# Two of four weight sums of a seven-product quad made by accumulating DMA on the GpSimd queue, and activations in 4 KB tiles of one pool (hybrid RG-LRU / attention layer, Trainium2)

## The chip, the cores and the metric

The kernel runs on one core of one Trainium2 chip. The metric is the device time of one execution in microseconds (us), as the median of several runs. Of the core's engines, PE multiplies matrices, VectorE (DVE in the profile) and ScalarE (ACT) work elementwise, GpSimd (POOL) does a few masks and issues some DMAs, and SyncE (SP) issues nearly all DMAs.

## The reference

One layer of a decoder trunk, 256 rows of 2048 features in float32, with an FFN of 5632 hidden features:

```python
mod = (c_act @ ada_w[l] + ada_b[l])[:, None, :]
sh1, sc1, g1, sh2, sc2, g2 = jnp.split(mod, N_MOD, axis=-1)
h = modulate(rms_norm(x, norm1_g[l]), sh1, sc1)
proj = h @ w_in[l] + b_in[l]
u, lru_gate, q, k, v, mix_gates = jnp.split(proj, SPLITS, axis=-1)
...
merged = gate_lru * (y_lru @ w_lru_out[l]) + gate_attn * (y_attn @ w_attn_out[l])
x = x + g1 * (merged @ w_o[l])
h2 = modulate(rms_norm(x, norm2_g[l]), sh2, sc2)
gate, up = jnp.split(h2 @ w_ffn_in[l], 2, axis=-1)
x = x + g2 * ((jax.nn.silu(gate) * up) @ w_ffn_out[l])
return rms_norm(x, final_g)
```

The elided part is a causal convolution, a gated linear recurrence and windowed attention. The change touches only the FFN's two products, the gate `g2` that the FFN needs at its end, and the tiles in which `h`, `h2` and the last rows lie.

## The kernel before, in words

**Products.** Every float32 operand is split into a rounded part `hi` and a remainder `lo`, and a product is three matmuls: hi by hi, hi by lo and lo by hi (`mm3`, L355 to L357; in the last stage written out at L1352). A weight block comes from HBM into a tile `raw` (128 x 1024, 512 KB), ScalarE casts it to `hi` (L305), and VectorE subtracts to get `lo` (L317).

**Order.** The program's order on every engine is the order in which the Python code emits it. All products are entries of a list `items`, and `step(i)` (L328) emits for item i, in this order: the loads up to item i+5, the weight sums `made` up to item i+4, the casts up to item i+3, the `lo` splits up to item i+2, the stages in `before`, and then the item's own matmuls. Three `lo` tiles, four `hi` tiles and five `raw` tiles go round, so a split waits for the matmuls of the item three before it. Work that is not on this path (normalisation, modulation, recurrence, attention) is cut into generators (`posts`, `sides`) and put between the items by a small model of the engines' clocks.

**Quads of seven.** At some places four neighbouring blocks of weights (two of the contraction, two of the output) and four of the activations form a quad, and `seven` (L397) makes their product with seven block products instead of eight. This needs four sums of weight blocks, each 128 x 512, and four of the activations. Two further items of the list are these weight sums: `first` (L418, L419) subtracts two pairs of raw blocks, `second` (L424, L425) goes on from there. VectorE makes all four; the results go the way of a raw block, through a cast and a split. In the FFN's first product (`add_pair`, output slabs 1 to 10) three of the eight pairs of contraction blocks are quads; `made` takes the two tiles of the tag `araw`. In the FFN's last product (`seven_last`) there are eight quads in each half of the output, taken in turn with plain pairs; there the sums lie in the tile `last`, which also holds the final rows and gain.

**The FFN's gate.** `ada_rows` computes the row of `g2`: 32 loads `aw` (512 KB each), each multiplied and added into `pa` by VectorE (L688), and then four matmuls `pb` on PE that sum over the partitions (L694), copied back by ScalarE (L696). `aw` uses the same two `araw` tiles and up to a few spare tiles of the pool `bp`. It runs as a side, and `all_modulations` finishes it ahead of output slab 1. Slab 0 is made plainly, by two slabs of eight items each: `fg` (gate half) and `fu` (up half).

**Tiles.** `h` and later `h2` lie in one tile of 32 KB in a pool of its own (`hp`), and after them `last` (32 KB). Everything else of 4 KB a partition lies in the pool `bp`, with 25 tiles.

Of the kernel before, what the change touches and what calls it, by code (L numbers as in the profile page):

```python
# [43 lines left out]

N_K = 1
# [17 lines left out]
N_MADE, N_HOLD = 5, 4  # L63
SEVEN = tuple(range(6, 36, 4))

SEVEN_1, SLAB_7 = (4, 8, 12), 1
EARLY = NH - 2 * N_HOLD

# [6 lines left out]
def hybrid_layer(  # L75
# [8 lines left out]
    hp = ctx.enter_context(tc.tile_pool(name="hp", bufs=1))  # L84
    bp = ctx.enter_context(tc.tile_pool(name="bp", bufs=N_B4))
# [191 lines left out]

    items = []
    live = {}
    at = {"load": 0, "made": 0, "hi": 0, "lo": 0}  # L280

    def do_load(i):
        src, cols = items[i].src, items[i].cols
        if callable(src):
            live[i] = [None, None, None, 0.0]
            return
        raw = wp.tile([P, CH], F32, tag="raw", name=f"raw{i}", bufs=AHEAD - 1)
        nc.sync.dma_start(raw[:, :cols], src)
        live[i] = [raw, None, None, load_time(cols)]

    def do_made(i):
        src = items[i].src
        if callable(src):
            clock["dve"] = max(clock["dve"], live[i - 1][3])
            live[i][0] = src(i)
            charge(1.2, 0)
            live[i][3] = clock["dve"]
# [29 lines left out]
    def step(i):  # L327
# [68 lines left out]

    SUMS = 4  # L397

    def seven(loads, where, act, bank, begin, end, made_in, post=None):

        got = {}

# [8 lines left out]
        def block(k, n):  # L411
            l, c0 = where[k, n]
            return got[l][:, c0:c0 + 512]

        def first(i):
            got.update({0: live[i - 2][0], 1: live[i - 1][0]})
            x = got["x"] = made_in(0)
            nc.vector.tensor_tensor(x[:, 0:512], block(0, 1), block(0, 0), op=ALU.subtract)  # L418
            nc.vector.tensor_tensor(x[:, 512:], block(0, 1), block(1, 1), op=ALU.subtract)  # L419
            return x  # L420

        def second(i):
            y, x = made_in(1), got["x"]
            nc.vector.tensor_tensor(y[:, 0:512], block(1, 1), x[:, 0:512], op=ALU.subtract)  # L424
            nc.vector.tensor_tensor(y[:, 512:], block(1, 0), y[:, 0:512], op=ALU.subtract)  # L425
            return y

        plain = ((0, (0, 0), "p"), (1, (1, 0), "00"), (6, (1, 1), "01"))
        for l in range(2):
            jobs = [(a, where[kn][1], to) for a, kn, to in plain if where[kn][0] == l]  # L430
            cs = [c0 for _, c0, _ in jobs]
            items.append(Item(
                loads[l], CH, products(*jobs), weight=0.25 * len(jobs), used=(min(cs), max(cs) + 512),
            ))
        items.append(Item(first, CH, products((3, 0, "r"), (5, 512, "u")), weight=0.5))
        items.append(Item(second, CH, products((4, 0, "q"), (2, 512, "10")), post, weight=0.5))

    def sums_of(to, a11, a12, a21, a22):

        s1, s2, s3, s4 = (to[:, i, :] for i in range(SUMS))  # L440
        nc.vector.tensor_tensor(s1, a21, a22, op=ALU.add)
        nc.vector.tensor_tensor(s3, a21, a11, op=ALU.subtract)
        nc.vector.tensor_tensor(s2, s1, a11, op=ALU.subtract)
        nc.vector.tensor_tensor(s4, a12, s2, op=ALU.subtract)
# [63 lines left out]
    h_both = hp.tile([P, NK, 2, S], F32R, tag="h", name="h_both")  # L508
    h_hi, h_lo = h_both[:, :, 0, :], h_both[:, :, 1, :]

    def hact(kt):
# [4 lines left out]
        return h_hi[:, kt, :], h_lo[:, kt, :]  # L516
# [17 lines left out]
    def h_low(kt):  # L534
        nc.vector.tensor_tensor(h_lo[:, kt, :], hx[kt], f32(h_hi[:, kt, :]), op=ALU.subtract)
        h_done.add(kt)

    def modulated():
        for kt in range(2):
# [6 lines left out]
            nc.scalar.copy(h_hi[:, kt, :], hx[kt])  # L546
            yield 0.33, 0
            h_low(kt)
        for kt in range(2, NK):
# [6 lines left out]
            nc.scalar.copy(h_hi[:, kt, :], hx[kt])  # L556
# [540 lines left out]
    def second_norm(banks):  # L1097
        sides[:] = [ada_ffn]
        clock["slack"] = SLACK[1]
        both = h2["both"] = hp.tile([P, NK, 2, S], F32R, tag="h", name="h2_both")  # L1100
        hh, hl = both[:, :, 0, :], both[:, :, 1, :]
# [38 lines left out]
        def high(p):  # L1140
            for j in range(2):
                kt = 2 * p + j
                nc.scalar.activation(hh[:, kt, :], x1T[p][:, j, :], AF.Identity, bias=modc[:, 3, kt:kt + 1])

        def low(p):
            for j in range(2):
                kt = 2 * p + j
                nc.vector.scalar_tensor_tensor(
                    hl[:, kt, :], x1T[p][:, j, :], modc[:, 3, kt:kt + 1], f32(hh[:, kt, :]),
# [42 lines left out]
    def h2act(kt):  # L1192
        return h2["both"][:, kt, 0, :], h2["both"][:, kt, 1, :]
# [39 lines left out]
    def add_pair(s):  # L1233
# [24 lines left out]
        def shared():  # L1258
# [9 lines left out]
            nc.vector.tensor_tensor(x[:, 1, :], banks["r"], g[:, 1, :], op=ALU.add)  # L1268
            nc.vector.tensor_tensor(x[:, 0, :], banks["r"], x[:, 0, :], op=ALU.add)
# [19 lines left out]
        for k in range(0, NK, 2):  # L1289
            loads = [w_f1[s + 11 * n][:, k * 512:(k + 2) * 512] for n in range(2)]  # L1290
            if k in SEVEN_1:
                last = k == SEVEN_1[-1]
                seven(
                    loads, {(0, 0): (0, 0), (1, 0): (0, 512), (0, 1): (1, 0), (1, 1): (1, 512)}, act(k), bank,
                    k == SEVEN_1[0], last,
                    lambda i: wp.tile([P, CH], F32, tag="araw", name="made", bufs=N_ADA), shared if last else None,
# [4 lines left out]
        if s == SLAB_7:  # L1301
            items[start].before.append(all_modulations)
# [16 lines left out]
    def last_first():  # L1319
        ada_ffn.finish(streams[-1].fetch)  # L1320
        last = hp.tile([P, 4, D], F32, tag="h", name="last")
        fin["x2"], fin["fg"], fin["made"] = last[:, 0:2, :], last[:, 2, :], last[:, 3, :]
        fin["ss"] = const.tile([P, 2, 5], F32, name="ss3")

# [6 lines left out]
    def fetch_last():  # L1331
        yield 0, 0
        nc.sync.dma_start(fin["fg"], fg_row.partition_broadcast(P))
        for t in range(2):
            yield 0, 0
            nc.sync.dma_start(fin["x2"][:, t, :], x1d[rows(t), :])
# [23 lines left out]
    def seven_last(k, n, src):  # L1360
        parts = {}

        def parts_high():
            hi = parts[0] = wp.tile([P, 8, P], F32R, tag="araw", name=f"ah{n}_{k}", bufs=N_ADA)
# [8 lines left out]
        def own(to):  # L1373
# [9 lines left out]
            (src[k], src[k + 1]), {(0, 0): (0, 0), (0, 1): (0, 512), (1, 0): (1, 0), (1, 1): (1, 512)},  # L1383
            lambda a: [parts[h][:, a, :] for h in range(2)], own, k == SEVEN[0], k == SEVEN[-1],
            lambda i: fin["made"][:, i * CH:(i + 1) * CH], (lambda: combined(n)) if k == SEVEN[-1] else None,
        )

    def combined(n):
# [16 lines left out]
        nc.vector.tensor_tensor(pqr, fin["r"], pq, op=ALU.add)  # L1405
        nc.vector.tensor_tensor(pqur, fin["r"], pqu, op=ALU.add)
# [11 lines left out]
    def add_block(t, ps, c0, cols, dst=None):  # L1418

        x2 = fin["x2"][:, t, c0:c0 + cols]  # L1420
# [12 lines left out]
    def blocks(n0, n1):  # L1433

        def post():
# [10 lines left out]
            for t in range(2):  # L1446
# [3 lines left out]
                x2 = fin["x2"][:, t, n0 * 512:n1 * 512]  # L1450
                nc.vector.tensor_tensor(x2, x2, fin["fg"][:, n0 * 512:n1 * 512], op=ALU.mult)
# [26 lines left out]
    def finish_first():  # L1478
# [223 lines left out]
```

## Time and profile before

| | |
|---|---|
| runs | 1550.64, 1551.02 and 1556.88 us, median 1551.02 |
| the profiled execution | 1549.47 us |
| its span, first to last instruction | 1547.7 us, mean granted PE clock 0.997 |
| busy | PE 1530.9, PE weight loads 1314.2, VectorE 1392.2, ScalarE 858.2, POOL 3.7 us |
| DMA | 400.37 MB, 259 GB/s over the span |
| chain that ended last | PE 93%, DMA 4%, DVE 2%, issue 1% |

Rows of the trace give the start in us from the first instruction, the duration in us, the engine, the line and operation, the tile written and the tiles read, and in brackets how long the engine stood idle before and what ended that. PE's matmuls overlap in the profile (one of 128 x 512 shows 0.39 us but the next one starts 0.23 later), so PE is read by starts, not by busy time. PEld is PE's weight load. In grouped rows the columns after the count are busy us, mean ns, and idle time before.

### The profile page before, as it was taken

The page shows a single profiled execution, that of the slowest core. Times are in us where ns is not written, and L with a number is a line of the kernel's source. Part 1 is how long each engine was busy: PE and PEld are TensorE (multiplying, and loading weights), DVE is VectorE, ACT ScalarE, POOL GpSimd, SP SyncE. Part 2 cuts the span into 40 slices and gives each one's busy share as a digit, 9 for nine tenths or more (in the row PEclk, how much of TensorE's full clock was granted, in tenths as well). Part 3 has the DMA queues.
Part 4 walks back from the last instruction along what each step waited for, and adds up shares of the span by engine and source line. Part 5 has one row for each costly group of instructions (what it writes and reads, how often), then busy time and mean ns, then how long its engine had stood idle before and what let it go on. Part 6 is the DMA issues. An engine that isn't in the chain of part 4 may idle for free.

```text
span 1547.7 us, 22116 instructions
## 1 busy us (share of the span) xinstructions
PE 1530.9 (99%) x8013; PEld 1314.2 (85%) x8013; DVE 1392.2 (90%) x1854; ACT 858.2 (55%) x1113; POOL 3.7 (0%) x11
## 2 busy tenths in 40 slices
PE   8999999999999999999999999999999999999997
PEld 7999999998878887888888788888888888888786
DVE  7889989889888887988988899999999999998998
ACT  4654443776855445444545655555555556664664
POOL 0000000000000000000000000000000000000000
PEclk9999999999999999999999999999999999999999
DMA  9999998666887797999999665565555666766563
GB/s 367 343 320 345 341 315 291 212 203 208 270 275 264 259 328 274 368 339 339 366 384 346 191 202 187 194 198 200 200 192 200 207 193 236 251 206 204 189 212 128
DMA packets 112909, 400.37 MB, mean 259 GB/s; under 512 B 12432, under 2 KB 12576, under 8 KB 112416
## 3 DMA queue, kind: packets, MB, share of 16 engines
q1 hardware_dynamic: 112192, 397.39, 74.5%
q8 instruction: 62, 1.02, 0.3%
q0 software_dynamic: 320, 1.06, 0.2%
q10 hardware_dynamic: 288, 0.52, 0.1%
q14 instruction: 47, 0.39, 0.1%
HBM read 394.72 MB, written 4.20 MB: 258 GB/s over the span
## 4 chain that ended last, share of the span: by engine, by line
PE 93%; DMA 4%; DVE 2%; issue 1%; ACT 0%; SPq 0%; DVEq 0%; ACTq 0%
PE pf L1352 9%; PE f L356 7%; PE f L357 7%; PE f L355 7%; PE wi L357 6%; PE wi L355 6%; PE wi L356 6%; PE wga L357 2%; PE wga L355 2%; PE wga L356 2%; PE wa L357 2%; PE wa L355 2%; PE wa L356 2%; PE wl L356 2%; PE wl L357 2%; PE wl L355 2%
## 5 line engine op out<-in xcount | busy, mean ns | idle before, releaser
L305 ACT CAST hi<-raw 128x1024 fp32r<-128x1024 f32 (+1 forms) x540 | 536.9, 1002 | 447.3 <-PE wi L356 77.2
L317 DVE TENSOR_TENSOR lo<-raw,hi 128x1024 fp32r<-128x1024 f32 (+1 forms) x540 | 618.7, 1159 | 66.0 <-issue 35.0
L357 PE MATMUL wi<-h_both,lo 128*128 128x256 f32 x800 | 227.3, 284 | 3.6 <-DVE lo L317 3.6
L355 PE MATMUL wi<-h_both,hi 128*128 128x256 f32 x800 | 228.0, 285 | 0.0
L356 PE MATMUL wi<-h_both,hi 128*128 128x256 f32 x800 | 227.0, 284 | 0.0
L355 PE MATMUL f<-hi,h_both 128*128 128x512 f32 x460 | 180.2, 392 | 0.0
L357 PE MATMUL f<-hi,h_both 128*128 128x512 f32 x460 | 179.0, 389 | 0.0
L356 PE MATMUL f<-lo,h_both 128*128 128x512 f32 x460 | 179.0, 389 | 0.0
L357 PEld LDWEIGHTS wi<-h_both,lo 128*128 128x128 f32 x800 | 154.2, 193 | 4.0 <-DVE lo L317 4.0
L356 PEld LDWEIGHTS wi<-h_both,hi 128*128 128x128 f32 x800 | 154.3, 193 | 0.2
L355 PEld LDWEIGHTS wi<-h_both,hi 128*128 128x128 f32 x800 | 154.3, 193 | 0.2
L305 ACT CAST hi<-made 128x1024 fp32r<-128x1024 f32 x60 | 63.4, 1057 | 112.8 <-PE f L357 111.3
L496 DVE CUSTOM_DVE_ANT_0 aw<-aw,crow,vec 128x1024 f32<-128x1024 f32 x79 | 100.6, 1278 | 6.2 <-DMA aw<-in_ada_t_dram 6.2
L496 DVE CUSTOM_DVE_ANT_0 aw<-aw,crow,modc 128x1024 f32<-128x1024 f32 x79 | 100.9, 1280 | 3.0 <-DMA aw<-in_ada_t_dram 2.8
L357 PEld LDWEIGHTS f<-hi,h_both 128*128 128x128 f32 x460 | 86.3, 188 | 18.0
L355 PEld LDWEIGHTS f<-hi,h_both 128*128 128x128 f32 x460 | 86.4, 188 | 17.8 <-issue 0.2
L356 PEld LDWEIGHTS f<-lo,h_both 128*128 128x128 f32 x460 | 86.4, 188 | 17.8 <-issue 0.2
L317 DVE TENSOR_TENSOR lo<-made,hi 128x1024 fp32r<-128x1024 f32 x60 | 73.4, 1225 | 25.9 <-PE f L356 20.7
L1352 PE MATMUL pf<-hi,fc 128*128 128x512 f32 x256 | 71.0, 389 | 0.0
L305 ACT CAST hi<-last 128x1024 fp32r<-128x1024 f32 x32 | 33.7, 1054 | 52.5 <-PE pf L1352 49.2
L1352 PEld LDWEIGHTS pf<-hi,fc 128*128 128x128 f32 x256 | 48.1, 188 | 10.0
L355 PE MATMUL wl<-hi,yh 128*128 128x512 f32 x128 | 52.5, 410 | 0.0
(355 smaller groups left out, 2940.4 us busy)
## 6 DMA issues: line engine op xcount, KB each, us to landing
raw<-in_w_f_dram SPq DMA_DIRECT2D x176, 512.0 KB, 4.2
raw<-in_w_in_dram SPq DMA_DIRECT2D x164, 512.0 KB, 7.1
aw<-in_ada_t_dram SPq DMA_DIRECT2D x158, 512.0 KB, 6.5
raw<-in_w_f2a_dram SPq DMA_DIRECT2D x44, 512.0 KB, 4.3
raw<-in_w_f2d_dram SPq DMA_DIRECT2D x36, 512.0 KB, 3.4
raw<-in_w_lru_dram SPq DMA_DIRECT2D x32, 512.0 KB, 6.5
raw<-in_w_att_dram SPq DMA_DIRECT2D x32, 512.0 KB, 7.8
raw<-in_w_o_dram SPq DMA_DIRECT2D x32, 512.0 KB, 8.3
```

Of the source, the lines that this page charges most:

```text
L305: nc.scalar.copy(hi[:, cs], live[i][0][:, cs])
L317: nc.vector.tensor_tensor(lo[:, cs], raw[:, cs], f32(hi[:, cs]), op=ALU.subtract)
L355: nc.tensor.matmul(ps, lhsT=lh, rhs=rh, start=start, stop=False, skip_group_check=True)
L356: nc.tensor.matmul(ps, lhsT=lh, rhs=rl, start=False, stop=False, skip_group_check=True)
L357: nc.tensor.matmul(ps, lhsT=ll, rhs=rh, start=False, stop=stop, skip_group_check=True)
L496: nc.vector.tensor_tensor_reduce(out=r, in0=r, in1=crow[:, j * CH:(j + 1) * CH], op0=ALU.mult, op1=ALU.add, scale=1.0, scalar=dst if j els ...
L1352: nc.tensor.matmul(bank(t, n), lhsT=l[:, rows(t)], rhs=w[:, c0:c0 + 512], start=kt == 0 and k == 0, stop=kt == (EARLY - 2 if (t, n) == (1, ...
```

## The change

It has four parts.

1. `seven`: two of the four weight sums are now made without VectorE. POOL's queue loads one raw block twice into a tile `wx` (two DMAs of 128 x 512, `fill`), and when they have landed loads two more blocks onto it with `accum_op=ALU.add` (`add`). `first` only hands this tile on. `second` makes the other two sums on VectorE into a tile `wy`, now by addition. Signs are turned accordingly in the sums of the activations (`sums_of`) and in those of the results (`shared`, `combined`). Of the second raw load of a quad only the half that is used is loaded.
2. `step` emits `fill` ten items and `add` seven items ahead of the item that uses it (N_SUM). `wx` uses the two `araw` tiles. So `all_modulations` is moved from the first item of slab 1 to seven items before it, the second item of `fu` (ALL_M). `ah`, which lay in an `araw` tile, now lies in a tile of `bp`.
3. `h` and `h2` are eight tiles of 4 KB in `bp`, which now has 33; the pool `hp` is gone.
4. The last rows and gain are six tiles of 4 KB, loaded by six DMAs of half a row each instead of three of whole rows.

```diff
+N_H = 8
+N_SUM = (11, 8)
+ALL_M = 7
...
-    hp = ctx.enter_context(tc.tile_pool(name="hp", bufs=1))
-    bp = ctx.enter_context(tc.tile_pool(name="bp", bufs=N_B4))
+    bp = ctx.enter_context(tc.tile_pool(name="bp", bufs=N_B4 + N_H))
...
+    def h_tiles(name):
+        ts = [bp.tile([P, 2, 2, S], F32R, tag="b4", name=f"{name}{i}") for i in range(N_H)]
+        return [[ts[kt // 2][:, kt % 2, i, :] for i in range(2)] for kt in range(NK)]
...
+    def do_sum(j):
+        def do(i):
+            if items[i].sums is not None:
+                items[i].sums[j]()
+                load_time(CH)
+        return do
...
-        nc.sync.dma_start(raw[:, :cols], src)
-        live[i] = [raw, None, None, load_time(cols)]
+        cs = items[i].used
+        nc.sync.dma_start(raw[:, cs], src)
+        live[i] = [raw, None, None, load_time(cs.stop - cs.start)]
...
+        upto("fill", do_sum(0), i + N_SUM[0])
+        upto("add", do_sum(1), i + N_SUM[1])
         for stage in it.before:
...
+        def fill():
+            x = got["x"] = wp.tile([P, CH], F32, tag="araw", name="wx", bufs=N_ADA)
+            for j in range(2):
+                nc.gpsimd.dma_start(x[:, j * 512:(j + 1) * 512], block(0, 1))
+
+        def add():
+            for j in range(2):
+                nc.gpsimd.dma_start(got["x"][:, j * 512:(j + 1) * 512], block(j, j), accum_op=ALU.add)
+
         def first(i):
-            got.update({0: live[i - 2][0], 1: live[i - 1][0]})
-            x = got["x"] = made_in(0)
-            nc.vector.tensor_tensor(x[:, 0:512], block(0, 1), block(0, 0), op=ALU.subtract)
-            nc.vector.tensor_tensor(x[:, 512:], block(0, 1), block(1, 1), op=ALU.subtract)
-            return x
+            return got["x"], 0

         def second(i):
-            y, x = made_in(1), got["x"]
-            nc.vector.tensor_tensor(y[:, 0:512], block(1, 1), x[:, 0:512], op=ALU.subtract)
-            nc.vector.tensor_tensor(y[:, 512:], block(1, 0), y[:, 0:512], op=ALU.subtract)
-            return y
+            def raw(*kn):
+                l, c0 = where[kn]
+                return live[i - 3 + l][0][:, c0:c0 + 512]
+
+            y = b4("wy", F32, (CH,))
+            free(b4=1)
+            nc.vector.tensor_tensor(y[:, 0:512], got["x"][:, 0:512], raw(1, 1), op=ALU.add)
+            nc.vector.tensor_tensor(y[:, 512:], y[:, 0:512], raw(1, 0), op=ALU.add)
+            return y, 1.3
...
-            items[start].before.append(all_modulations)
+            items[start - ALL_M].before.append(all_modulations)
...
-        last = hp.tile([P, 4, D], F32, tag="h", name="last")
-        fin["x2"], fin["fg"], fin["made"] = last[:, 0:2, :], last[:, 2, :], last[:, 3, :]
+        for h in range(2):
+            fin["fg", h] = bp.tile([P, CH], F32, tag="b4", name=f"fg{h}")
+            for t in range(2):
+                fin["x2", t, h] = bp.tile([P, CH], F32, tag="b4", name=f"x2{t}{h}")
...
-            hi = parts[0] = wp.tile([P, 8, P], F32R, tag="araw", name=f"ah{n}_{k}", bufs=N_ADA)
+            hi = parts[0] = b4(f"ah{n}_{k}", F32R, (8, P))
```

Two places show how instructions move. The first is the end of slab 0. On VectorE before, in the second half of `fu`, splits (`lo`), rows of the gate (`pa`) and sums for the activations' quads (`hs`) alternate; the numbers behind the names tell tiles apart:

```order
L317 TENSOR_TENSOR lo_8376<-raw_8313,hi_8353 128x1024
L688 SCALAR_TENSOR_TENSOR pa<-aw_8015,cact,pa 128x1024
L317 TENSOR_TENSOR lo_8399<-raw_8333,hi_8374 128x1024
L688 SCALAR_TENSOR_TENSOR pa<-aw_8036,cact,pa 128x1024
L441 TENSOR_TENSOR hs_8414<-x1T_8168 128x128
L442 TENSOR_TENSOR hs_8414<-x1T_8168 128x128
L443 TENSOR_TENSOR hs_8414<-hs_8414,x1T_8168 128x128
L444 TENSOR_TENSOR hs_8414<-x1T_8168,hs_8414 128x128
L317 TENSOR_TENSOR lo_8423<-raw_8351,hi_8397 128x1024
L317 TENSOR_TENSOR lo_8443<-raw_8372,hi_8421 128x1024
L688 SCALAR_TENSOR_TENSOR pa<-aw_8075,cact,pa 128x1024
```

On VectorE now, at the same place:

```order
L337 TENSOR_TENSOR lo_8387<-raw_8324,hi_8364 128x1024
L719 SCALAR_TENSOR_TENSOR pa<-aw_8019,cact,pa 128x1024
L337 TENSOR_TENSOR lo_8410<-raw_8344,hi_8385 128x1024
L719 SCALAR_TENSOR_TENSOR pa<-aw_8040,cact,pa 128x1024
L719 SCALAR_TENSOR_TENSOR pa<-aw_8079,cact,pa 128x1024
L719 SCALAR_TENSOR_TENSOR pa<-aw_8190,cact,pa 128x1024
L719 SCALAR_TENSOR_TENSOR pa<-aw_8224,cact,pa 128x1024
L719 SCALAR_TENSOR_TENSOR pa<-aw_8251,cact,pa 128x1024
L719 SCALAR_TENSOR_TENSOR pa<-aw_8303,cact,pa 128x1024
L473 TENSOR_TENSOR hs_8442<-x1T_8179 128x128
```

Five rows of `pa` have moved up, so that six stand on end behind one split. On PE before, the four sums `pb` come between the last item of `fu` and the first of slab 1 (`f_1`):

```order
L356 MATMUL fu_0_1_8379<-lo_8484,h_both 128x512
L357 MATMUL fu_0_1_8379<-hi_8461,h_both 128x512
L694 MATMUL pb_8553<-pa,ones 128x512
L694 MATMUL pb_8556<-pa,ones 128x512
L694 MATMUL pb_8559<-pa,ones 128x512
L694 MATMUL pb_8562<-pa,ones 128x512
L355 MATMUL f_1_8565<-hi_8482,h_both 128x512
```

On PE now, between the first item of `fu` (it reads the tile `h_0`) and the second (`h_1`):

```order
L378 MATMUL fu_0_1_8390<-lo_8348,h_0_8093 128x512
L379 MATMUL fu_0_1_8390<-hi_8326,h_0_8093 128x512
L725 MATMUL pb_8418<-pa,ones 128x512
L725 MATMUL pb_8421<-pa,ones 128x512
L725 MATMUL pb_8424<-pa,ones 128x512
L725 MATMUL pb_8427<-pa,ones 128x512
L377 MATMUL fu_0_0_8389<-hi_8346,h_1_8094 128x512
```

`pb` has moved up by seven items, past the rest of `fu`. The second place is a quad. On VectorE before, the second quad of slab 1:

```order
L317 TENSOR_TENSOR lo_8689<-raw_8639,hi_8678 128x1024
L317 TENSOR_TENSOR lo_8701<-raw_8663,hi_8687 128x1024
L418 TENSOR_TENSOR made<-raw_8685,raw_8676 128x512
L419 TENSOR_TENSOR made<-raw_8685 128x512
L317 TENSOR_TENSOR lo_8715<-raw_8676,hi_8699 128x1024
L424 TENSOR_TENSOR made<-raw_8685,made 128x512
L425 TENSOR_TENSOR made<-raw_8676,made 128x512
L317 TENSOR_TENSOR lo_8736<-raw_8685,hi_8713 128x512
L317 TENSOR_TENSOR lo_8754<-made,hi_8734 128x1024
L317 TENSOR_TENSOR lo_8766<-made,hi_8752 128x1024
```

On VectorE now, the same quad:

```order
L337 TENSOR_TENSOR lo_8707<-raw_8655,hi_8694 128x1024
L337 TENSOR_TENSOR lo_8719<-raw_8679,hi_8705 128x1024
L337 TENSOR_TENSOR lo_8730<-raw_8692,hi_8717 128x1024
L454 TENSOR_TENSOR wy<-wx,raw_8703 128x512
L455 TENSOR_TENSOR wy<-wy,raw_8692 128x512
L337 TENSOR_TENSOR lo_8754<-raw_8703,hi_8728 128x512
L337 TENSOR_TENSOR lo_8772<-wx,hi_8752 128x1024
L337 TENSOR_TENSOR lo_8784<-wy,hi_8770 128x1024
```

Two sums are gone, the other two read `wx`. On POOL's queue, whose last DMAs before were the three of the gate `g1`, the quads now follow one after the other, fill before add (`wx_8492` is the first quad's tile):

```order
L1052 DMA g11_7191<-g1d_175 128x1024
L438 DMA wx_8492<-in_w_f1_dram 128x512 x2
L442 DMA wx_8492<-in_w_f1_dram 128x512 x2
L438 DMA wx_8634<-in_w_f1_dram 128x512 x2
L442 DMA wx_8634<-in_w_f1_dram 128x512 x2
```

An add waits for its fill to land, and a fill waits for VectorE and ScalarE to be done with the tile of the quad before last.

More of the change, by code (lines that the diff above doesn't have):

```diff
@@ L276, in __init__ @@
             self.used, self.before = slice(*(used or (0, cols))), list(before)
+            self.sums = None
     items = []
     live = {}
-    at = {"load": 0, "made": 0, "hi": 0, "lo": 0}
+    at = {"fill": 0, "add": 0, "load": 0, "made": 0, "hi": 0, "lo": 0}
+    def do_sum(j):
[4 more added lines that the diff above has]
+        return do
     def do_load(i):
@@ L397, in hybrid_layer, with seven @@
     SUMS = 4
-    def seven(loads, where, act, bank, begin, end, made_in, post=None):
+    def seven(loads, block, by_k, act, bank, begin, end, post=None):
         got = {}
+        where = {(k, n): (k, n * 512) if by_k else (n, k * 512) for k in range(2) for n in range(2)}
         def products(*jobs):
@@ L430, in seven @@
             jobs = [(a, where[kn][1], to) for a, kn, to in plain if where[kn][0] == l]
-            cs = [c0 for _, c0, _ in jobs]
+            cs = [where[kn][1] for _, kn, _ in plain if where[kn][0] == l]
+            used = (min(cs), max(cs) + 512)
             items.append(Item(
-                loads[l], CH, products(*jobs), weight=0.25 * len(jobs), used=(min(cs), max(cs) + 512),
+                loads[l][:, slice(*used)], CH, products(*jobs), weight=0.25 * len(jobs), used=used,
             ))
         items.append(Item(first, CH, products((3, 0, "r"), (5, 512, "u")), weight=0.5))
+        items[-1].sums = fill, add
         items.append(Item(second, CH, products((4, 0, "q"), (2, 512, "10")), post, weight=0.5))
@@ L505, in ada_cols @@
                 cols_done.add((m, kt))
-    h_both = hp.tile([P, NK, 2, S], F32R, tag="h", name="h_both")
-    h_hi, h_lo = h_both[:, :, 0, :], h_both[:, :, 1, :]
+    h = h_tiles("h")
     def hact(kt):
@@ L1099, in second_norm @@
         clock["slack"] = SLACK[1]
[L1100 to L1101 removed]
+        hh = h2["parts"] = h_tiles("h2_")
         for p in range(4):
@@ L1293, in add_pair @@
                 seven(
-                    loads, {(0, 0): (0, 0), (1, 0): (0, 512), (0, 1): (1, 0), (1, 1): (1, 512)}, act(k), bank,
-                    k == SEVEN_1[0], last,
-                    lambda i: wp.tile([P, CH], F32, tag="araw", name="made", bufs=N_ADA), shared if last else None,
+                    loads, lambda j, n, k=k: w_f1[s + 11 * n][:, (k + j) * 512:(k + j + 1) * 512], False, act(k), bank,
+                    k == SEVEN_1[0], last, shared if last else None,
                 )
@@ L1332, in fetch_last @@
         yield 0, 0
-        nc.sync.dma_start(fin["fg"], fg_row.partition_broadcast(P))
-        for t in range(2):
+        for h in range(2):
+            cs = slice(h * CH, (h + 1) * CH)
+            for t in range(2):
+                nc.sync.dma_start(fin["x2", t, h], x1d[rows(t), cs])
             yield 0, 0
-            nc.sync.dma_start(fin["x2"][:, t, :], x1d[rows(t), :])
+            nc.sync.dma_start(fin["fg", h], fg_row[cs].partition_broadcast(P))
+            yield 0, 0
     def out_products(jobs, t2=(0, 1), hold=None, after=None):
```

80 lines of the change are left out of this document (41 added, 39 removed).

## The prediction

> **What bounds the kernel now.** I read the page first: busy shares by slice, then the chain that ended last.
>
> ```profile
> PE   8999999999999999999999999999999999999997
> DVE  7889989889888887988988899999999999998998
> PE 93%; DMA 4%; DVE 2%; issue 1%; ACT 0%; SPq 0%; DVEq 0%; ACTq 0%
> ```
>
> PE is on the chain for 93% of the span and VectorE for 2%, although VectorE is nine tenths busy in the second half, where every quad of seven products lies. So the second question is whether PE ever waits there. The busy time by stage (columns: length, then PE, PEld, DVE, ACT and POOL busy, clock, DMA share, GB/s) says it does not in a slab of the FFN's first product, and this holds for all the slabs I looked at; the first row is the projection stage, kept for its DMA rate.
>
> ```profile
> 440.00:816.00 376.00, 375.07 (x1687) 306.80 (x1686) 331.76 (x461) 181.34 (x268) 1.70 (x3) 1.00 0.91 321
> 1033.00:1075.00 42.00, 42.00 (x191) 34.88 (x190) 39.26 (x48) 24.00 (x28) 0.00 (x0) 1.00 0.60 200
> ```
>
> PE 42.00 of 42.00, VectorE 39.26 of 42.00. Busy spans of PE overlap, so I checked the spacing in the chain, where one quad and one plain pair of the last stage take one step.
>
> ```profile
> 1324.93 5.44 PE pf L1352 x24
> 1335.13 5.44 PE pf L1352 x24
> ...
> 1449.97 5.44 PE pf L1352 x24
> ...
> 1460.70 5.44 PE pf L1352 x24
> ...
> 1470.99 5.44 PE pf L1352 x24
> 1481.19 5.44 PE pf L1352 x24
> ```
>
> The step is 10.20 us (1324.93 to 1335.13). It is longer twice, 10.73 (1449.97 to 1460.70) and 10.29, beside the seam between the two halves of the last stage. PE's own rows add the step before these.
>
> ```profile
> 1439.10 0.62 PE L1352 MATMUL pf<-hi,fc 128*128 128x512 f32 x2
> ...
> 1449.81 0.62 PE L1352 MATMUL pf<-hi,fc 128*128 128x512 f32 x2
> ```
>
> That one is 10.71. Everywhere else the step is PE's own work: 24 matmuls in 5.44 us.
>
> **Part 1, the removed sums.** Each quad loses two of its four VectorE sums, 30 quads in the slabs and 16 in the last stage (the groups of one of the four lines):
>
> ```profile
> L418 DVE TENSOR_TENSOR made<-raw,raw 128x512 f32<-128x512 f32 x30 | 20.5, 684 | 0.0
> ...
> L418 DVE TENSOR_TENSOR last<-raw 128x512 f32<-128x512 f32 x16 | 11.0, 685 | 0.0
> ```
>
> That is 92 instructions of 0.68 us, 55 to 63 us less for VectorE (they follow each other every 0.60). PE waits for VectorE only in the three long steps, so all that can come back is 0.51 + 0.53 + 0.09 = 1.1 us. The rest turns into idle time of VectorE. The signs that are turned in the later sums cost nothing: same instruction, same size. **-1.1 us** (bounds 0 and -1.1).
>
> **Part 2, the gate's rows finished earlier.** `made` was taken from the two `araw` tiles, and `wx` is now, its fill emitted six items ahead of where the sums were; so `all_modulations` must have emptied these tiles seven items sooner (ALL_M). The order shows what follows: after the first item of the slab `fu`, PE now has the four `pb` matmuls, and VectorE has six `pa` rows on end before them, where one was. In the trace of before these rows were spread among the splits (VectorE):
>
> ```profile
> 862.03 1.23 DVE L317 TENSOR_TENSOR lo<-raw,hi 128x1024 fp32r<-128x1024 f32 x1 [0.30 <-ACT x1T L1165]
> 863.17 1.28 DVE L688 SCALAR_TENSOR_TENSOR pa<-aw,cact,pa 128x1024 f32<-128x1024 f32 x1
> 864.37 0.28 DVE L441 TENSOR_TENSOR hs<-x1T 128x128 f32<-128x128 f32 x1
> ...
> 879.65 1.28 DVE L688 SCALAR_TENSOR_TENSOR pa<-aw,cact,pa 128x1024 f32<-128x1024 f32 x1
> ```
>
> and PE came to `pb` when they were done (PE):
>
> ```profile
> 861.77 0.39 PE L357 MATMUL fu<-hi,h_both 128*128 128x512 f32 x1
> 862.00 0.39 PE L355 MATMUL fu<-hi,h_both 128*128 128x512 f32 x1
> ...
> 880.81 0.39 PE L357 MATMUL fu<-hi,h_both 128*128 128x512 f32 x1
> 881.04 3.59 PE L694 MATMUL pb<-pa,ones 128*128 128x512 f32 x8
> ```
>
> 881.04 follows 880.81 at the usual 0.23, so nothing was waited for. In the changed order PE is through with the first `fu` item at 862.00. VectorE's split of 862.03 stands ahead of the six rows and cannot start sooner, because it writes the `lo` tile that this same item has just read. The rows then start at 863.17 and follow every 1.20 (863.17 to 864.37). The first `pb` needs the half of `pa` that the fifth row completes: 863.17 + 4 x 1.20 + 1.28 = 869.25. PE has nothing else in its queue and stands from 862.00 to 869.3, **+7.3 us**; the sixth row ends at 870.45, under the first two `pb`. The loads are no cause of more: the last of them was issued by 847.3 and the slowest took 9.4.
>
> ```profile
> L467 SPq DMA_DIRECT2D aw<-in_ada_g_dram x9: 327/422/911, 815.2 to 847.3; - x9
> ...
> DMA to landing us min/median/max: 4.4/7.5/9.4
> ```
>
> `pb` itself costs the same 3 us at either place. Behind the six rows on VectorE stand the sums of `hs` and the split for the fifth `fu` item; three items are split already, 8 us of matmuls, so that queue is late for nobody. On ScalarE the four copies of `pb` wait for PE with the next cast behind them, for which PE has four items in hand.
>
> An idle PE also loses its clock. The last matmul of the kernel starts at 1539.02; the granted clock (column before the DMA share) is 0.97 two microseconds later and 0.50 after that.
>
> ```profile
> 1541.00:1543.00 2.00, 0.00 (x0) 0.00 (x0) 1.58 (x5) 0.87 (x2) 0.00 (x0) 0.97 0.26 100
> 1543.00:1545.00 2.00, 0.00 (x0) 0.00 (x0) 0.00 (x0) 0.00 (x0) 0.00 (x0) 0.50 0.99 385
> ```
>
> 0.97 over 2 us is a halving at 1542.9, some 3.6 us after PE stopped. What a restart costs shows at the start of the kernel, where durations tell more than the clock column (min/median/max in ns):
>
> ```profile
> 1.06 2.93 PE L150 MATMUL warm<-ones 128*128 128x128 f32 x12 [1.06 <-DVE eps_t L142]
> ...
> 9.11 3.51 PE L150 MATMUL warm<-ones 128*128 128x128 f32 x30
> ```
>
> ```profile
> L167 PE MATMUL c_ps<-crow,ones x8: 592/592/1219, 4.3 to 8.7; 128*128 128x512 f32 x8
> ```
>
> The first warm-up matmuls take 244 ns each, the later ones 117; `c_ps`, the same shape as `pb`, begins at 1219 and ends at 592. Taking full speed from the middle of these eight, 6.5, the slow phase lasts 5.4 us from 1.06, half of it lost. For a stop of 7.3 us, twice the 3.6, I take that row whole: **+2.7 us** (bounds 0 and 2.7). The Trainium skill, TensorE: Matmul & The Clock Gate (Part 1: The HAM clock gate), says that one idle window of about 3.4 us halves the clock and about one busy window restores it; the 3.6 us above agrees, and by its restart the loss would be 1.7 us, an estimate from that page, and the sum 1 us lower.
>
> **Part 3, the loads on POOL's queue.** Per quad two fills and two accumulating loads of 256 KB come, and SP loads 256 KB less: 46 x 0.79 MB = 36 MB more. In a slab that is 2.4 MB in 42.4 us, 56 GB/s on top of 200, still below the 321 GB/s at which PE was 375.07 of 376.00 busy. POOL has no other work there, so its wait between fill and add keeps back only the next fill. `wx` waits for VectorE's split of the quad before last, two steps or 20.4 us earlier; after it has landed VectorE has two sums, a half split and the split of `wx` to do before the tile is free again. Their starts in a quad of before:
>
> ```profile
> 956.16 0.69 DVE L424 TENSOR_TENSOR made<-raw,made 128x512 f32<-128x512 f32 x1
> 956.88 0.70 DVE L425 TENSOR_TENSOR made<-raw,made 128x512 f32<-128x512 f32 x1
> 957.49 0.69 DVE L317 TENSOR_TENSOR lo<-raw,hi 128x512 fp32r<-128x512 f32 x1
> ```
>
> 1.33 us for the two, 0.6 for the half and 1.23 for the whole split (862.03) are 3.2 us, so fill and add together may take 20.4 - 3.2 = 17.2 us unnoticed. No accumulating load is in the trace. The nearest rows are the two plain loads on POOL's queue and the loads of SP:
>
> ```profile
> L1021 POOL DMA_DIRECT2D g<-g1d x2: 527/541/555, 727.3 to 727.9; - x2
> ...
> DMA to landing us min/median/max: 7.2/8.6/10.0
> ```
>
> ```profile
> raw<-in_w_f_dram SPq DMA_DIRECT2D x176, 512.0 KB, 4.2
> ...
> raw<-in_w_att_dram SPq DMA_DIRECT2D x32, 512.0 KB, 7.8
> ```
>
> Two issues of 0.54 and a landing of 4.2 us, twice, make 10.6 us; with the slowest POOL landing, 10.0, it is 22.2. POOL's 8.6 stood beside SP's 7.8 in the same busy stage, a tenth more, so I take 11.4, six under the limit: **0 us**. The cover is that reserve; without it each microsecond over 17.2 costs about 18 (below).
>
> **Part 4, the tiles.** `h` and the last rows in 4 KB tiles, `ah` in a tile of that pool, and the loads of x1 and the final gain in six halves instead of three rows: same bytes, same instructions on PE and ScalarE. SP already waited for PE before the first of these loads, with raw loads behind it, and no step of the chain there was longer:
>
> ```profile
> SPq L1333 <- PE f L357: 3.8, 1, 3.8
> ```
>
> No row prices the rest; I take 0 and allow 1 us either way, also for waits of SP's loads that now name other buffers in the first 840 us.
>
> **Sum.** The profiled execution took 1549.47 us (span 1547.7 and 1.8 around it): 1549.5 - 1.1 + 7.3 + 2.7 = 1558.4. The median of the runs shown, 1551.02, lies 1.55 above that execution, so I predict 1559.9.
>
> **Rivals.** (a) Not slower than a measurement can tell, 0.5% or 7.8 us: the stop is there, but the clock holds or recovers at once. Stop less gain is 6.2 us, so this is decided at a clock loss of 1.6; with none the time is 1557.2. For it: the loss rests on the start of the kernel, where PE was fed sparsely. Against: 7.3 is twice the 3.6 after which the clock fell. (b) POOL becomes the pace: fill and add over 17.2 us. At 22.2 the excess is 5.0 for each pair of quads that are 20.4 apart, one per slab and eight in the last stage, 18 x 5.0 = 90 us, so 1650; at 18 us it is 14, so 1574. For it: an accumulating load must also read its destination, and VectorE is nine tenths busy, with POOL building the loads beside it. The Trainium skill, SBUF — State Buffer (SBUF: two separate sides), warns of this: a DMA from POOL's queue can starve while VectorE is in a two-port mode. Against, from the rows above: the two loads of 727.3 issued in 0.54 us each and landed almost like SP's. (c) Faster: VectorE's 55 us come back somewhere that the profile hides. At most the 2% of the chain, some 30 us, were VectorE's, most of it before 840 us, which the change does not touch; I give 1543 with a small chance.
>
> **Chances.** The forecast 0.50, (a) 0.33, (b) 0.13, (c) 0.04. Part of the forecast's spread and all of (a) count as no change, so: faster 0.04, same 0.38, slower 0.58. The range runs from 1554, (a) less the untracked microseconds and the run's own spread, to 1575, which takes in (b) up to 18 us; left out are the rest of (b) and (c).
>
> **What would show it.** Right: between the first and second `fu` item a gap of about 7 us on PE that ends with a `pa` row, a granted clock under 1 behind it, `pb` at about 870 instead of 881, and from there on steps of 10.20 with no long one at the seam. Wrong: no gap there; waits of the `wy` sums or of ScalarE's casts for `wx` in quad after quad (then (b)); or steps under 10.20.

## The result and the profile after

| | before | after |
|---|---|---|
| median of 11 runs each, on one chip | 1551.43 us | 1559.72 us |
| ratio, 95% interval | | 1.0048 [1.0033, 1.0063] |
| the profiled execution | 1549.47 us (span 1547.7) | 1560.67 us (span 1558.9) |
| DMA | 400.37 MB | 436.58 MB |
| VectorE busy | 1392.2 us | 1343.0 us |

The changed kernel is 8.3 us slower by the medians (0.53%); the ratio, estimated from all the runs, says 0.48%. Two executions of the experiments below, one of 1689.21 and one of 1899.10 us, ran in a slower state with a granted clock of 0.85 and 0.75, and the medians and ratios given there leave them out. The page of after, busy tenths by slice, the clock and the chain that ended last:

```profile
PE   8999999999999999999999899999999999999997
DVE  7889989899888888998988688888888888888988
PEclk9999999999999999999999899999999999999999
PE 93%; DMA 3%; DVE 2%; ACT 1%; issue 1%; SPq 0%; DVEq 0%; ACTq 0%
```

VectorE has become a tenth emptier in most slices of the second half, as it should. PE has not gained anything by it: its row has the same nines, and a new 8 in the slice from about 857 to 896 us, where the clock has an 8 too. The items of `fu` lie in that slice. PE's rows there:

```profile
863.39 0.39 PE L379 MATMUL fu<-hi,h 128*128 128x512 f32 x1
870.90 6.78 PE L725 MATMUL pb<-pa,ones 128*128 128x512 f32 x8 [7.13 <-DVE pa L719]
877.11 0.80 PE L377 MATMUL fu<-hi,h 128*128 128x512 f32 x1
```

PE is through with the first item of `fu` at 863.62 (863.39 and the usual 0.23), then waits for the rows of `pa` until 870.90: 7.28 us. VectorE's rows say why, six rows on end behind one split:

```profile
863.65 1.23 DVE L337 TENSOR_TENSOR lo<-raw,hi 128x1024 fp32r<-128x1024 f32 x1 [0.30 <-ACT x1T L1195]
864.79 7.26 DVE L719 SCALAR_TENSOR_TENSOR pa<-aw,cact,pa 128x1024 f32<-128x1024 f32 x6
871.96 0.29 DVE L473 TENSOR_TENSOR hs<-x1T 128x128 f32<-128x128 f32 x1
```

Behind the stop `pb` takes 6.21 us (870.90 to 877.11). The busy time in stretches of 2 us shows the granted clock, the third number from the end:

```profile
864.00:866.00 2.00, 0.00 (x0) 0.00 (x0) 2.00 (x3) 0.86 (x1) 0.00 (x0) 1.00 0.69 221
866.00:868.00 2.00, 0.00 (x0) 0.00 (x0) 2.00 (x3) 0.00 (x0) 1.07 (x2) 0.72 0.72 234
868.00:870.00 2.00, 0.00 (x0) 0.00 (x0) 2.00 (x3) 0.00 (x0) 0.00 (x0) 0.50 0.73 256
...
876.00:878.00 2.00, 2.00 (x6) 0.97 (x5) 0.00 (x0) 0.87 (x2) 0.00 (x0) 0.72 0.63 219
878.00:880.00 2.00, 2.00 (x10) 1.67 (x9) 0.00 (x0) 0.30 (x1) 1.05 (x2) 1.00 0.05 18
```

A mean of 0.72 over 2 us is a halving at 866.9, 3.3 us after PE stopped, and a return at 877.1, 6.2 us after it started again. Further on, the same slab's window and the chain through the last stage:

```profile
1033.00:1075.00 42.00, 42.00 (x191) 34.89 (x190) 35.81 (x42) 23.98 (x28) 8.77 (x12) 1.00 0.88 257
```

```profile
1325.92 0.87 PE ft L988 x8
...
1451.24 5.44 PE pf L1392 x24
1461.44 5.44 PE pf L1392 x24
1471.64 5.44 PE pf L1392 x24
...
1522.64 21.76 PE pf L1392 x96
```

PE is still 42.00 of 42.00 busy in a slab, now with VectorE at 35.81 instead of 39.26 and the DMA share at 0.88 instead of 0.60. At the seam, between the two halves of the last stage, every step is 10.20 now. From the last `ft` to the final 96 matmuls it is 196.72 us (1522.64 - 1325.92), and it was 197.94, by these two rows of the chain of before:

```profile
1313.85 0.87 PE ft L957 x8
...
1511.79 21.76 PE pf L1352 x96
```

That is the gain, 1.22 us. So the theory is: the stop (7.3) and the cold clock behind it cost some 10 us, the sums give 1.2 back, and the loads on POOL's queue cost nothing. The rival: the denser DMA traffic and the tiles have a share in the loss, and would keep it if the stop were gone.

### The profile page after: what moved, and what is told of

Its sections match the earlier page's. It is cut to its first block, busy times and chain, and to the rows that moved or that the text cites. A ratio compares the mean times of both kernels' runs of the same rounds, so it can differ in the third digit from the quotient of the medians.

```text
span 1558.9 us, 22364 instructions
## 1 busy us (share of the span) xinstructions
PE 1534.2 (98%) x8013; PEld 1315.8 (84%) x8013; DVE 1343.0 (86%) x1762; ACT 858.5 (55%) x1113; POOL 138.0 (9%) x195
## 2 busy tenths in 40 slices
DMA packets 133951, 436.58 MB, mean 280 GB/s; under 512 B 15424, under 2 KB 15568, under 8 KB 133840
## 4 chain that ended last, share of the span: by engine, by line
PE 93%; DMA 3%; DVE 2%; ACT 1%; issue 1%; SPq 0%; DVEq 0%; ACTq 0%
PE pf L1392 9%; PE f L379 7%; PE f L378 7%; PE f L377 7%; PE wi L379 6%; PE wi L377 6%; PE wi L378 6%; PE wl L378 2%; PE wga L378 2%; PE wga L377 2%; PE wga L379 2%; PE wa L378 2%; PE wa L379 2%; PE wa L377 2%; PE wl L379 2%; PE wl L377 2%
## 5 line engine op out<-in xcount | busy, mean ns | idle before, releaser
L379 PE MATMUL wi<-h,lo 128*128 128x256 f32 x800 | 227.3, 284 | 3.7 <-DVE lo L337 3.7
L377 PE MATMUL wi<-h,hi 128*128 128x256 f32 x800 | 228.0, 285 | 0.0
L378 PE MATMUL wi<-h,hi 128*128 128x256 f32 x800 | 227.0, 284 | 0.0
L377 PE MATMUL f<-hi,h 128*128 128x512 f32 x460 | 179.8, 391 | 0.0
L379 PE MATMUL f<-hi,h 128*128 128x512 f32 x460 | 179.0, 389 | 0.0
L378 PE MATMUL f<-lo,h 128*128 128x512 f32 x460 | 179.0, 389 | 0.0
L379 PEld LDWEIGHTS wi<-h,lo 128*128 128x128 f32 x800 | 154.2, 193 | 4.1 <-DVE lo L337 4.1
L378 PEld LDWEIGHTS wi<-h,hi 128*128 128x128 f32 x800 | 154.3, 193 | 0.2
L377 PEld LDWEIGHTS wi<-h,hi 128*128 128x128 f32 x800 | 154.3, 193 | 0.2
L337 DVE TENSOR_TENSOR lo<-wx,hi 128x1024 fp32r<-128x1024 f32 x46 | 56.4, 1225 | 58.3 <-PE f L378 42.2
L379 PEld LDWEIGHTS f<-hi,h 128*128 128x128 f32 x460 | 86.4, 188 | 17.9
L378 PEld LDWEIGHTS f<-lo,h 128*128 128x128 f32 x460 | 86.4, 188 | 17.6
L377 PEld LDWEIGHTS f<-hi,h 128*128 128x128 f32 x460 | 86.4, 188 | 17.5
L337 DVE TENSOR_TENSOR lo<-wy,hi 128x1024 fp32r<-128x1024 f32 x46 | 56.4, 1225 | 8.9 <-ACT hi L325 4.5
```

The lines of the kernel that those rows point to most:

```text
L337: nc.vector.tensor_tensor(lo[:, cs], raw[:, cs], f32(hi[:, cs]), op=ALU.subtract)
L377: nc.tensor.matmul(ps, lhsT=lh, rhs=rh, start=start, stop=False, skip_group_check=True)
L378: nc.tensor.matmul(ps, lhsT=lh, rhs=rl, start=False, stop=False, skip_group_check=True)
L379: nc.tensor.matmul(ps, lhsT=ll, rhs=rh, start=False, stop=stop, skip_group_check=True)
```

## Experiments

**Only the move.** The kernel before, with one line changed:

```diff
-            items[start].before.append(all_modulations)
+            items[start - 7].before.append(all_modulations)
```

> The kernel before with one edit: all_modulations seven items earlier, at the second item of fu. No loads on POOL's queue, no new tiles. Theory (the move alone is the loss): 1551.4 + 7.3 + 3.2 = 1561.9 us, with the stop in front of pb at 862 to 869.3 and the clock at 0.50 behind it. Rival (the loss comes with the loads or the tiles): 1551 to 1554 us.

Measured: 1561.46 us against 1550.60 of before, ratio 1.0070 [1.0053, 1.0088]. PE's rows:

```profile
865.28 0.39 PE L357 MATMUL fu<-hi,h_both 128*128 128x512 f32 x1
872.79 6.34 PE L694 MATMUL pb<-pa,ones 128*128 128x512 f32 x8 [7.13 <-DVE pa L688]
878.57 0.80 PE L355 MATMUL fu<-hi,h_both 128*128 128x512 f32 x1
```

The same stop to the hundredth (865.51 to 872.79 is 7.28) with no load on POOL's queue; `pb` takes 5.78. The clock falls here too:

```profile
866.00:868.00 2.00, 0.00 (x0) 0.00 (x0) 2.00 (x3) 0.75 (x1) 0.00 (x0) 0.98 0.69 219
...
878.00:880.00 2.00, 2.00 (x8) 1.27 (x7) 0.00 (x0) 1.17 (x2) 0.00 (x0) 0.96 0.00 0
```

By the same working it is halved from 867.9 to 878.2, so 2.4 us after PE stopped and until 5.4 us after it started again. The low stretch lasts 10.2 us, as in after (866.9 to 877.1). The move alone makes at least the whole loss, and the seam keeps its long steps:

```profile
1327.40 0.87 PE ft L957 x8
...
1525.31 21.76 PE pf L1352 x96
```

197.91 us, as in before. These rows also tell what a shift in one pair of traces is worth: the first item of `fu` ended at 865.51 here, at 862.00 in before, and the order of the program up to there is the same. Three or four microseconds before 860 are spread between executions.

**The rows early, `pb` late.** The changed kernel, where only VectorE's rows are finished early:

```diff
-            items[start - ALL_M].before.append(all_modulations)
+            items[start - ALL_M].before.append(all_rows)
+            items[start].before.append(all_modulations)
...
-            yield 0, 0, 0, 1
+            yield 0, 0, 0, 1, lambda: "pb" in ready
```

> The changed kernel with only the rows of the gate (pa) finished at the second item of fu, and the four matmuls pb and their copies left at the first item of slab 1, where they stood before. Theory (the whole loss is PE's stop in front of pb, 7.3 us, and the cold clock behind it, 3.2 us; the loads on POOL's queue cost nothing): PE no longer waits for the rows. But the rows still stand on end on VectorE in front of the split of the fifth item of fu: they end at about 872.0, the four hs sums take 1.2 and the split 1.2, so 874.5, and PE has three split items from 863.6 on, 7.7 us, to 871.3. A stop of about 3.2 us stays, too short for the clock to fall: 1559.7 - 7.3 - 3.2 + 3.2 = 1552.4 us. Rival (the loads and the denser DMA cost at least half of the loss, spread over the slabs): 1556 us or more.

Measured: 1552.80 us against 1550.60, ratio 1.0011 [0.9999, 1.0023]. Six of the eight microseconds are back with the loads on POOL's queue still in place, and the rival falls. The 2.2 that stay have an interval of -0.2 to 3.6, so the short stop of 3.2 that was expected may be there; no row here shows it.

**The rows spread too.** Two rows of `pa` in each of the three items before, so that one is left:

```diff
+            for i in range(ALL_M + 1, ALL_M + 4):
+                items[start - i].before.append(two_rows)
             items[start - ALL_M].before.append(all_rows)
...
```

> As e1_pb_later, and the rows spread: two rows in each of the three items before, so that only one is left at the second item of fu, no two splits further apart than two rows. Theory: no stop at all, the clock stays: 1559.7 - 10.5 = 1549.2 us, that is 2.2 us (0.14%) less than before the change, from the three long steps at the seam that are gone (1.1 us). Rival (the loads cost time in the slabs): 1556 us or more, and steps longer than 10.20 or waits for wx in the slabs.

Measured: 1550.30 us against 1550.60, ratio 1.0001 [0.9989, 1.0012]. In PE's rows of `fu` one wait is left:

```profile
869.15 0.50 PE L378 MATMUL fu<-lo,h 128*128 128x512 f32 x1 [0.23 <-DVE lo L337]
```

and the chain shows slabs of 42.37 us (973.76 to 1016.13; `ft` are the transposes that end a slab) and, from the last `ft` on, the gain at the seam again, 196.73 us:

```profile
973.76 0.87 PE ft L989 x8
1016.13 0.87 PE ft L989 x8
...
1312.75 0.88 PE ft L989 x8
...
1509.48 21.76 PE pf L1410 x96
```

A slab of before takes the same 42.37 us:

```profile
974.86 0.87 PE ft L957 x8
1017.23 0.87 PE ft L957 x8
```

So the other three parts of the change together cost nothing that shows, within the 1.8 us of the interval. The 1.2 us of gain are in the trace, but too small for the medians.

**PE kept busy in the stop.** Small matmuls of ones in front of `pb`, first 60, then 30:

```diff
+        yield 0, 0, 0, 1
+        keep_warm(60)
         for c in range(4):
```

> The changed kernel with 60 small matmuls of ones (128x128, 117 ns each warm, 7.0 us) on PE in front of pb, so that PE is busy while it waits for the rows. This separates the stop from the clock. Theory (stop 7.3, clock loss 3.2): the stop stays, the clock does not fall, pb takes 3.0 instead of 6.2 us: 1559.7 - 3.2 = 1556.5 us. Rival (the clock has no part in it: pb is slow behind the stop for another reason, such as ScalarE's copies of pb, which stand between casts): 1559.7 us or more, with pb still over 6 us though the clock shows 1.00.

Measured: 1562.52 us, ratio 1.0082 [1.0063, 1.0101]. The time went up instead of down, because the expectation had mis-sized the filler: such a matmul shows as two rows in the profile, so that 60 take 13.4 us and PE came to `pb` late. But `pb` is as short as in before, 3.04 us:

```profile
860.62 13.56 PE L160 MATMUL warm<-ones 128*128 128x128 f32 x120
874.01 3.60 PE L727 MATMUL pb<-pa,ones 128*128 128x512 f32 x8
877.05 0.80 PE L377 MATMUL fu<-hi,h 128*128 128x512 f32 x1
```

```diff
-        keep_warm(60)
+        keep_warm(30)
```

> As e3_keep_warm with half as many matmuls. There each of the 60 took two rows of the profile at 113 ns, 13.4 us in all and not 7.0, so that PE reached pb 4.3 us later than the rows needed; pb itself took 3.0 us at clock 1.00. With 30 of them PE is busy for 6.7 of the 7.3 us of the stop. Theory (clock loss 3.2, stop 7.3): 1559.7 - 3.2 = 1556.5 us. Rival (no clock loss to be had back): 1559.7.

Measured: 1558.06 us against 1550.36, ratio 1.0047 [1.0032, 1.0062].

```profile
864.51 6.86 PE L160 MATMUL warm<-ones 128*128 128x128 f32 x60
871.80 3.70 PE L727 MATMUL pb<-pa,ones 128*128 128x512 f32 x8 [0.43 <-DVE pa L719]
874.94 0.79 PE L377 MATMUL fu<-hi,h 128*128 128x512 f32 x1
```

The stop is the same, 7.29 us (864.51 to 871.80), and `pb` takes 3.14 instead of 6.21: the clock's share is 3.07 us in the trace. The medians, 7.7 us over before here and 8.3 for the changed kernel in another series, are too coarse to show it.

**POOL loaded more.** Every fill made twice:

```diff
+            for _ in range(2):
                 for j in range(2):
                     nc.gpsimd.dma_start(x[:, j * 512:(j + 1) * 512], block(0, 1))
```

> The changed kernel with every fill of wx made twice, the second behind the first's landing. Fill to add is 4.8 us in the last stage, add to landing about 7, so 12 us for both; a second fill makes 16.9. Theory of the prediction (the tile: fill and add may take 17.2 us): no change, 1559.7 us, at most 2 us more. Rival (POOL's queue in its order: the next fill stands behind the add, so fill to fill is 4.8 + 1.8 = 6.6 us of POOL per quad now, 11.4 with the second fill, over the 10.20 us of a step in the last stage): 1.2 us for each of 16 quads less the lead of some 5 us, so 1559.7 + 14 = 1574 us; the slabs, with three quads in 42.4 us, stay.

Measured: 1636.38 us against 1550.36, ratio 1.0542 [1.0518, 1.0567]. Both expectations are far too low. Some 23 us of the loss lie in the slabs, which the rival had left as they are: from the first slab's transposes to the tenth's it is 405.1 us (942.0 to 1347.1) instead of 382.1 in after (944.4 to 1326.5). POOL's rows in the last stage (L439 fills, L443 adds):

```profile
1386.13 1.80 POOL L443 DMA_DIRECT2D wx<-in_w_f2a_dram  x2 [2.75 <-DMA wx<-in_w_f2a_dram]
1387.48 1.57 POOL L439 DMA_DIRECT2D wx<-in_w_f2a_dram  x2
1396.57 1.19 POOL L439 DMA_DIRECT2D wx<-in_w_f2a_dram  x2 [7.52 <-DMA wx<-in_w_f2a_dram]
1399.99 1.80 POOL L443 DMA_DIRECT2D wx<-in_w_f2a_dram  x2 [2.24 <-DMA wx<-in_w_f2a_dram]
```

The fill at 1387.48 follows its neighbour's add without any wait, so the tile was long free and POOL's queue itself is the pace: 13.86 us from add to add (1386.13 to 1399.99), where a step has 10.20. The queue rule holds, and its price was wrong: a fill issued right behind two adds takes 9 us until the next DMA may go (1387.48 to 1396.57), not the 4.8 of a fill into an idle queue.

**Using VectorE's free time.** Since the slabs are PE's, what VectorE no longer does is worth something only if PE gets less work. A fourth quad per slab saves PE 0.68 us. First on the kernel before, where VectorE makes all four sums:

```diff
-SEVEN_1, SLAB_7 = (4, 8, 12), 1
+SEVEN_1, SLAB_7 = (2, 6, 10, 12), 1
...
-            if k in SEVEN_1:
-                last = k == SEVEN_1[-1]
+            mine = SEVEN_1[1:] if s == SLAB_7 else SEVEN_1
+            if k in mine:
+                last = k == mine[-1]
...
```

> The same fourth quad in the kernel before, where VectorE makes all four sums. It stands as the counterpart of e8_fourth_quad. Theory (VectorE has no room without the relief): a slab costs VectorE 39.3 us; a quad in place of a plain pair adds four sums of 0.65, four splits (1.2, 0.6, 1.2, 1.2) for two of 1.2, so 4.4 us, to 43.7 in a slab of 41.7. VectorE sets the pace of slabs 2 to 10: 1.3 us each over the old 42.4, 1550.6 + 12 = 1562 us, less what the splits ahead buffer. Rival (VectorE is not near its limit): 1544.5 us as in e8.

Measured: 1577.78 us, ratio 1.0182 [1.0164, 1.0200]. VectorE is now busy 43.11 of 45.00 us:

```profile
1030.00:1075.00 45.00, 43.24 (x189) 34.14 (x188) 43.11 (x55) 25.36 (x30) 0.00 (x0) 1.00 0.56 187
```

It needs more time than the 41.69 us that PE would take for a slab. The direction of the theory holds, but not its size, 12 us: over nine slabs the transposes lie 409.2 us apart (939.7 to 1348.9), 27 us more than in before (932.3 to 1314.4), which is the whole loss. Of these, 9.9 us are nine waits of PE at the quad behind the transposes; the rest was not taken apart. The same edit on the version with the rows spread, two of the four sums on POOL's queue:

> e2_rows_spread with a fourth quad of seven in slabs 2 to 10 (contraction blocks 2, 6, 10, 12 in place of 4, 8, 12; slab 1 keeps three, 6, 10 and 12). Each quad saves PE one block product, 3 matmuls of 0.227 us. Theory (VectorE's relief is real but was unused; POOL and DMA have room): 9 x 0.68 = 6.1 us less than e2: 1550.3 - 6.1 = 1544.2 us, slabs of 41.7 instead of 42.4 us. Rival (the loads are no longer free: DMA share 0.88 rises to about 0.95, and between quads 6 and 12 only 15 us lie, less 3.2 leaves 11.8 for fill and add, which take about 12): 1550 us or more, with waits for wx or raw.

Measured: 1560.15 us, ratio 1.0071 [1.0052, 1.0090]. Slower than with three quads, as the rival said, but 17.6 us faster than its counterpart. PE's row behind the transposes `ft` points to one cause, the PSUM banks (where PE's results lie) that the quad's `fu` needs and that `fc` has not read yet:

```profile
936.83 0.47 PE L377 MATMUL fu<-hi,hs 128*128 128x512 f32 x1 [0.66 <-DVE fc L1258]
```

There are nine such waits, 5.9 us in all, of the 16 us by which the kernel misses the theory; its chain also runs through late loads of `wx` in three slabs. The quads were moved, in all ten slabs, so that the extra line for slab 1 goes:

```diff
-SEVEN_1, SLAB_7 = (2, 6, 10, 12), 1
+SEVEN_1, SLAB_7 = (4, 6, 10, 12), 1
```

> e2_rows_spread with four quads per slab at the contraction blocks 4, 6, 10, 12 in all ten slabs. In e8_fourth_quad PE stood about 1.5 us per slab behind the transposes ft, where the quad at block 2 needs their two PSUM banks before ScalarE and VectorE have read them, and up to 1.3 us at the quad at block 12, whose wx landed late. Here no quad follows ft. Theory (the banks were most of it): 10 x 0.68 = 6.8 us gained, up to 0.3 us per slab lost at the two places where the same wx tile comes back after 15 us instead of 20.4: 1550.3 - 6.8 + 3 = 1546.5 us. Rival (POOL's loads are the limit: two places per slab now have only 11.8 us for fill and add): 1.3 us at each of them, 26 us in ten slabs, so 1570 us.

Measured: 1576.14 us, ratio 1.0164 [1.0151, 1.0178]. The rival was nearer; what the banks cost can't be told beside it. The chain of waits now runs through the loads of `wx` in nearly every slab:

```profile
1047.58 7.32 DMA wx<-in_w_f_dram
1054.99 1.05 ACT hi L325
1056.07 1.24 DVE lo L337
1057.35 0.50 PE fr L378
```

On top of it a third tile:

```diff
-AHEAD, N_HI, N_LO, N_ADA, N_B4 = 6, 4, 3, 2, 25
+AHEAD, N_HI, N_LO, N_ADA, N_B4 = 6, 4, 3, 3, 24
```

> e10_fourth_quad_moved with a third wx tile (and one tile fewer in the general pool), so that a fill no longer waits for the split of the quad before last. The gate's loads use the third tile too. Theory (what e10 loses is the wait for the tile): the two late places go, 1550.3 - 6.8 = 1543.5 us. Rival (POOL's queue in its order or the DMA rate is the limit, not the tile): no better than e10.

Measured: 1549.44 us against 1551.24, ratio 0.9990 [0.9981, 0.9998]. The third tile takes back 27 us, so the wait for the tile was the main cause in the version before it. A slab is 42.04 us by two rows of the chain, 0.33 less than the 42.37 of three quads, where 0.68 were to be had; where the other half goes stays open, and the time stays 6 us over the theory's 1543.5:

```profile
929.41 0.87 PE ft L989 x8
971.45 0.87 PE ft L989 x8
```

This is the one version here that is faster than both kernels, by 0.1% over before, about 2 us, with an interval that only just leaves out no difference.

## Why the prediction was right, point by point

**Direction and sum.** Predicted 8.9 us more than the profiled execution of before; the medians give 8.3. That the forecast of 1559.9 lies 0.2 from the median of after is luck: the interval of the result alone is 4.7 us wide, and the clock's term was 0.5 off. By its size alone the result lies on the border that rival (a) drew, 7.8 us; the traces decide between the two. The terms measured on the traces are 7.3 for the stop, 3.2 for the clock and -1.2 at the seam, 9.3 in all. The profiled execution of after lies 11.2 over that of before; 1.6 of the rest is there already when the first item of `fu` ends (863.62 and 862.00), where executions of one order differ by more, as the move alone showed.

**Part 1, -1.1.** The long steps at the seam are gone, 1.22 us. The rest of VectorE's 49 us (1392.2 to 1343.0, where 55 to 63 had been counted) turned into idle time, as said. The pair with quads at 2, 6, 10 and 12 shows that they can be worth something once PE has less work: with the four sums on VectorE a fourth quad costs 27 us, with two of them on POOL's queue 10. The pair does not split this 17 into VectorE's own time and PE's waits at the transposes, which shrink too (9.9 to 5.9).

**Part 2, the stop, +7.3.** Measured 7.28, in two kernels. The step behind it was the order: six rows on end on VectorE, and `pb` next on PE. Leaving `pb` where it was took away most of the loss; spreading the rows took the rest, as far as the medians tell.

**Part 2, the clock, +2.7, bounds 0 and 2.7.** The mechanism was right; the size was 3.2 in after and 2.7 in the kernel with the move alone (6.21 and 5.78, less the 3.04 of a warm PE), so the upper bound was set too low. What the prediction missed is that the loss depends on where the stop falls: the clock was low for 10.2 us in both, but fell 3.3 us after PE's stop in one and 2.4 in the other, and half of the time from `pb` to its return (6.2 and 5.4) is the loss. That 2.7, read off the start of the kernel, meets one of them exactly is luck. Rival (a), a clock loss under 1.6, falls with both. The Trainium skill, TensorE: Matmul & The Clock Gate (Part 1: The HAM clock gate), says that an idle window of about 3.4 us halves the clock; the 3.3 us of after agree with that figure, and the 2.4 of the move alone are less. It gives about one busy window for the way back; the traces have 6.2 and 5.4 us from the first matmul on, and the measurement decides.

**Part 3, 0 us.** The grouped rows of the fills and of the adds in after:

```profile
L438 POOL DMA_DIRECT2D wx<-in_w_f_dram x60: 541/567/1117, 866.4 to 1291.8; - x60
...
DMA to landing us min/median/max: 2.9/4.6/6.8
```

```profile
L442 POOL DMA_DIRECT2D wx<-in_w_f_dram x60: 877/898/1242, 870.7 to 1295.7; - x60
...
DMA to landing us min/median/max: 4.3/7.6/11.2
```

A fill lands in 4.6 us, about as fast as SP's plain loads of before (4.2). An accumulating load takes 0.90 us to issue and 7.6 to land, more than the 4.6 taken for it. From fill to add lie 4.8 us in the last stage (1353.81 to 1358.64, for one), 0.9 later the second add goes out, 7.6 later it has landed: 13.3 us instead of 11.4, still under the 17.2 that the tile allows. That rule gives the right size for the kernel with quads at 4, 6, 10 and 12: twice per slab the tile comes back after 15.0 us instead of 20.4, 11.8 are left, and 1.5 us at 20 places are 30; the third tile, which takes this wait away, gave back 26.7. What the prediction missed is the second limit. It said that POOL's wait between fill and add keeps back only the next fill. The doubled fills show that the queue is a limit of its own, about as near: it has 10.20 us per quad in the last stage and uses about 6.6, so 3.6 are spare where the tile has 3.9, and a fill that must follow the adds at once is twice as slow. Rival (b) did not come about, but at less distance than its number said. What it took from the Trainium skill, SBUF — State Buffer (SBUF: two separate sides), that a DMA from POOL's queue can starve while VectorE is in a two-port mode, no run here shows: VectorE was 85% busy in the slabs and a fill was issued in 0.57 us, much as POOL's loads of before (0.54).

**Part 4, 0.** The kernel with the rows spread has these tiles and the time of before, with an interval of 0.12% either way, so this term, within that interval, is right as well.

## What to carry to other kernels

Work that is taken off an engine is worth what that engine made the pacing engine wait, here 1.2 of 49 us; more can come only if the pacing engine's work is cut along with it. A change that takes over a buffer moves whatever must empty the buffer first, and every instruction of that step moves along, so look for the one on the pacing engine's in-order queue (here `pb`) and separate it from the rows that really have to move. An in-order DMA queue with a wait between two DMAs has a throughput limit of its own beside the limit of its tiles; check both before counting its reserve.

## What the runs showed of the hardware

- PE's clock fell 3.3 us after the last matmul in one execution and 2.4 in another, came back 6.2 and 5.4 us after the next one, and was low for 10.2 us in both; a stop of 7.3 us cost 10.5 and 10.0.
- Small matmuls in the stop keep the clock at 1.00: `pb` then took 3.0 to 3.1 us instead of 5.8 to 6.2.
- Of the loads of 256 KB on POOL's queue in the slabs of after, an accumulating one is issued in 0.90 us and lands in 7.6 (median, 11.2 at most), a plain one in 0.57 and 4.6; a plain one issued right behind two accumulating ones, in the kernel with doubled fills, held its successor for 9 us.
- 36 MB more, a DMA share of 0.88 instead of 0.60 in the slabs, cost PE nothing that can be measured: a slab took 42.37 us with and without.
